# Low halves of the up-projection's weights: from a VectorE subtraction to a ScalarE negation and an accumulating DMA on GpSimd's queue

## The chip, the cores and the metric

The kernel runs on one core of a Trainium2 chip. The metric is the device time of one execution in microseconds (us), less is better. The kernel before takes 1237.1 us, the median of 2 runs (1236.72 to 1237.47).

The engines of a core are named as in the profile: PE (TensorE, the matmuls), PEld (its weight loads), DVE (VectorE), ACT (ScalarE), POOL (GpSimd) and SP (SyncE, which only issues transfers here). Each engine works through its own instructions strictly in order. DMA queues are fed by SP ("SPq"), POOL ("POOLq") and ACT ("ACTq"), and 16 DMA engines move the data.

## The reference

A trunk of two layers on one sequence of 512 tokens with D = 1024: layer 0 mixes tokens with attention with a forget gate, layer 1 with a gated short convolution. Each mixer is followed by the MLP, which is what the change touches, and by a gated embedding.

```python
def sq_relu_mlp(h, w_up, w_down):          # w_up (1024, 4096), w_down (4096, 1024)
    return jnp.square(jax.nn.relu(h @ w_up)) @ w_down

for i in range(DEPTH):                     # DEPTH = 2
    ...
    x = x + rmsnorm(m, g[1])               # m: the mixer's output
    f = sq_relu_mlp(rmsnorm(x, g[2]), w_up[i], w_down[i])
    x = x + rmsnorm(f, g[3])
    ...
```

All inputs and the output are float32.

## The kernel before, in words

**Numbers in two parts.** Every operand of a large matmul is kept as two tiles of the type float32r: hi, the value rounded, and lo, what the rounding left (value minus hi). `mm3` (L262) issues three products for one: hi by hi (L264), lo by hi (L265), hi by lo (L266). `split` (L270) makes the two parts: ScalarE writes hi with a copy that rounds (L272), and an engine, DVE unless told otherwise, writes lo as source minus hi (L273). In the profile L272 is the line of all casts and L273 that of all subtractions; the tiles are told apart by name (wh and wl for weights, hTh and hTl for the normed activations, S1h, A12l and so on for the down-projection's right-hand sides).

**The stream of weights.** All weights come from HBM as tiles of 128x512 float32, 256 KB each, in one planned list. `plan` and its relatives write `loads` (what to load) and `order` (what to prepare). `fetch` (L157) issues the loads on SP's queue into a ring of 14 raw buffers (`RAWS`, tiles "raw"); a buffer can be loaded again when its last reader is done with it. `prepare` (L170) goes through `order`: it fetches the tile, takes two pages (wh, wl) from a pool and calls `split`. `wide` and `narrow` are called by the matmul loops and prepare 8 tiles (`SOON`) ahead.

**The MLP.** For each layer 8 groups of 512 hidden channels. A group has 8 raw tiles of the up-projection (key "up"); there are 128 such tiles in all. `up` makes four blocks f = 0 to 3 of hidden activations: for each, eight steps k with `mm3`, then Relu (L825) and Square on ACT. For groups 0 to 6 the down-projection is computed with seven products instead of eight (`plan_down`, `down`): besides the four quarters B11, B12, B21, B22 of the weight block, it needs the sums T1 to T4 of them, made in `derive` (L167, tiles dn_T) by POOL, eight per group, and the low parts of these sums are also made by POOL (`prepare` chooses `nc.gpsimd` for derived "dn" tiles, so wl<-dn_T at L273). On the other side, `quarters` (L839) has POOL form four sums s of the activations per half group, eight per group, from which ACT and DVE then make S1h, S1l and so on. `down` adds each product onto an accumulator with DVE (L871). `combine` (L878) has POOL add the seven accumulators into the output after group 6, 14 additions per layer, while group 7 ("up" and an ordinary "dn") runs.

**Around the MLP.** The norms: squares on ACT (L295, into "junk"), two small operations on POOL (L287, L290, tiles n_r, cor_r, or_r and mr_r), scaling on DVE (L303, n_h), transposes on PE (L312, n_p), then `split` into hT.

**What sets the order.** The Python order of the statements isn't the order of the engines: the tile framework schedules the whole program by a timeline of its own (`schedule_with_timeline_sim=True`), places each instruction on its engine, and adds the waits between engines. Each engine then runs its list in that order.

Of the kernel before, what the change touches and what calls it, by code (L numbers as in the profile page):

```python
# [11 lines left out]
ALU = mybir.AluOpType  # L12
# [56 lines left out]
def trunk(ctx: ExitStack, tc, x, pT, g, wv, wqk, bf, wo, wci, wcq, cw, wco, wup, wdn, wpp, wpg, out):  # L69
    nc = tc.nc  # L70
# [9 lines left out]
    def page(name, dtype=F32):  # L80
        return pages.tile([P, S], dtype, tag="pg", name=name)
# [69 lines left out]
    def fetch(upto):  # L151
        while len(fetched) < min(upto, len(loads)):
            n = len(fetched)
            raw = raws.tile([P, S], F32, tag="raw", name=f"raw{n}")
            fetched.append(raw)
            src = loads[n]
            nc.sync.dma_start(raw[:, : src.shape[-1]], src)  # L157

    def derive(key):
        at, sums = recipes.pop(key)  # L160
        fetch(max(at.values()) + 1)
        B = {name: fetched[n][:, :S] for name, n in at.items()}
        for name, a, b, op in sums:
            t = page("_".join(str(u) for u in (*key, *name)))
            derived[(*key, *name)] = t
            B[name] = t[:, :S]
            ins = nc.gpsimd.tensor_tensor(out=B[name], in0=B[a], in1=B[b], op=op)  # L167
            if last_norm:
                tc.add_manual_dep(
                    ins.ins, last_norm.pop().ins.name,  # L170
                    mybir.DependencyInfo(mybir.DependencyClass.Sync, mybir.DependencyReason.DATA),
                )

    def prepare(upto):
        while begun[0] < min(upto, len(order)):
            n = begun[0]
            begun[0] += 1
            key, at = order[n]
            for of in (key[:3], key[:2]):
                if of in recipes:  # L180
                    derive(of)
            hi, lo = page(f"wh{n}", F32R), page(f"wl{n}", F32R)
            if isinstance(at, tuple):
                raw, w = derived.pop(key), S
                eng = nc.gpsimd if key[0] == "dn" or key[-1] in ON_POOL else nc.vector
            else:
                fetch(at + 1)
                raw, eng, w = fetched[at], nc.vector, loads[at].shape[-1]
                fetched[at] = None
            split(hi[:, :w], lo[:, :w], raw[:, :w], eng)  # L190
            ready[key] = Pair(hi[:, :w], lo[:, :w])

    def wide(*key, soon=SOON):

        prepare(where[key] + 1 + soon)
        return ready[key]
# [73 lines left out]
    def split(hi, lo, src, eng=nc.vector):  # L270

        nc.scalar.copy(hi, src)  # L272
        eng.tensor_tensor(out=lo, in0=src, in1=hi.bitcast(F32), op=ALU.subtract)  # L273
# [96 lines left out]
    def mixer_out(kind, lhs, xs, gB, then, opened):  # L370


        mgs, sums = {}, {}
        for t, n in BLOCKS:
            if (t, n) == (2, 0):
                prepare(where[kind, 1, KT - 1] + 1 + SOON)
            at = (t, n) in opened
            ps = opened.pop((t, n)) if at else bank(f"{kind}{n}_{t}")
            for k in range(KT - 1 if at else 0, KT):
                mm3(ps, lhs(k, t), wide(kind, n, k, soon=soon(t, n)), k == 0, k == KT - 1)  # L380
            sums[t, n] = squares(ps, f"{kind}s{n}_{t}")
            mgs[t, n] = gained(ps, gB, n, f"{kind}m{n}_{t}")
            if (t, 1 - n) in mgs:
                residual(t, *([d.pop((t, i)) for i in range(2)] for d in (mgs, sums)), xs[t],
                         f"{kind}r")
                then(t)

    def attention(hT, first_x, g0, by_hand):
# [212 lines left out]
        def stream():  # L601
            for i in range(1, KT):
                yield from project(i)
            yield from out_part((0,), range(6))
            yield from out_part((1,), range(6))
            prepare(where["o", 1, KT - 1] + 1)
            yield from out_part((0, 1), (6,))
# [499 lines left out]
```

## Time and profile before

| | |
|---|---|
| median of 2 runs | 1237.1 us |
| span of the profiled execution | 1235.8 us |
| that execution beside the median | 1.3 us shorter (span only) |
| PE busy | 1213.4 us |
| DVE, ACT, POOL busy | 896.5, 676.1, 686.8 us |
| bytes moved by DMA | 148.73 MB |

The numbers of an engine are the time in which it executes. A row of the groups view gives line, engine, operation, output<-inputs, shapes and count, then total busy time and mean ns of one, then the engine's idle time ahead of these instructions and whom it waited for. A row of the timeline gives start and duration in us, and in brackets the idle time before it and its releaser; "x4" is four alike in a row. The waits view gives, for a pair of lines, the time waited in total, how often, and the longest. A row with min/median/max lists the durations in ns of one tile's instructions.

### The profile page before, as it was taken

Reading aid. Unit: us, or ns where it says so; the run is one execution under the profiler, and the core shown is the slowest. Engines: PE = TensorE matmul, PEld = TensorE weight load, DVE = VectorE, ACT = ScalarE, POOL = GpSimd, SP = SyncE. Lnnn points to the kernel's source line nnn. Section 1 sums busy time; section 2 is a strip of 40 time slices with the busy share of each in tenths; the row PEclk is TensorE's granted clock in tenths of the full one; section 3 lists DMA queues with packets and bytes.
Section 4 is the critical chain, followed back from the end, with each engine's and each line's share of the span. In section 5 each row is a group of like instructions: output and inputs, shape, how many; then the busy total and the mean of one; then the engine's idle time right before and its main releaser. Section 6 shows DMA issues by size and latency. Waiting matters only on the chain.

```text
span 1235.8 us, 18684 instructions
## 1 busy us (share of the span) xinstructions
PE 1213.4 (98%) x6188; PEld 1030.6 (83%) x6188; DVE 896.5 (73%) x1394; ACT 676.1 (55%) x1429; POOL 686.8 (56%) x667
## 2 busy tenths in 40 slices
PE   7999999999999999999999999999999999999997
PEld 6888888888888888888889999989778888888885
DVE  5657878675667667869877798865767787669873
ACT  5457777556635654465566544445756345635551
POOL 2016667247878777775213255317778868778210
PEclk9999999999999999999999999999999999999999
DMA  7456564442343224428133033552412443235401
GB/s 253 150 160 169 147 159 114 151 164 66 115 137 98 88 88 136 123 69 288 67 102 107 27 107 96 154 176 71 136 59 78 137 136 95 66 114 178 163 18 52
DMA packets 85793, 148.73 MB, mean 120 GB/s; under 512 B 10112, under 2 KB 17328, under 8 KB 85696
## 3 DMA queue, kind: packets, MB, share of 16 engines
q1 hardware_dynamic: 85488, 147.27, 38.7%
q8 instruction: 49, 0.80, 0.3%
q14 instruction: 48, 0.39, 0.1%
q10 hardware_dynamic: 144, 0.26, 0.1%
q0 software_dynamic: 64, 0.00, 0.0%
HBM read 136.93 MB, written 6.37 MB: 116 GB/s over the span
## 4 chain that ended last, share of the span: by engine, by line
PE 89%; DVE 3%; POOL 2%; ACT 2%; issue 2%; DMA 2%; SPq 0%; POOLq 0%; DVEq 0%; ACTq 0%
PE up L266 9%; PE up L265 9%; PE up L264 9%; PE dn L265 8%; PE dn L266 8%; PE dn L264 8%; PE pg L265 2%; PE pg L264 2%; PE pg L266 2%; PE qk L264 2%; PE qk L265 2%; PE qk L266 2%; PE co L264 1%; PE co L266 1%; PE co L265 1%
## 5 line engine op out<-in xcount | busy, mean ns | idle before, releaser
L273 DVE TENSOR_TENSOR wl<-raw,wh 128x512 fp32r<-128x512 f32 (+1 forms) x398 | 370.2, 975 | 27.5 <-ACT wh L272 26.3
L272 ACT CAST wh<-raw 128x512 fp32r<-128x512 f32 (+1 forms) x398 | 217.1, 620 | 4.6 <-DVE xd L348 4.4
L265 PE MATMUL up<-hTh,wl 128*128 128x512 f32 (+1 forms) x576 | 210.2, 365 | 0.0
L266 PE MATMUL up<-hTl,wh 128*128 128x512 f32 (+1 forms) x576 | 209.7, 366 | 0.3 <-DVE hTl L273 0.3
L264 PE MATMUL up<-hTh,wh 128*128 128x512 f32 (+1 forms) x576 | 209.4, 366 | 0.0
L273 POOL TENSOR_TENSOR wl<-dn_T,wh 128x512 fp32r<-128x512 f32 x112 | 155.0, 1417 | 32.6 <-ACT wh L272 32.6
L825 ACT ACTIVATE r<-up 128x512 f32<-128x512 f32 (+1 forms) x72 | 39.4, 547 | 200.4 <-PE up L266 200.4
L871 DVE TENSOR_TENSOR acc<-dn,acc 128x512 f32<-128x512 f32 x168 | 107.2, 678 | 23.9 <-PE dn L266 23.9
L265 PEld LDWEIGHTS up<-hTh,wl 128*128 128x128 f32 x576 | 108.6, 189 | 17.7
L264 PEld LDWEIGHTS up<-hTh,wh 128*128 128x128 f32 x576 | 108.6, 189 | 17.5
L266 PEld LDWEIGHTS up<-hTl,wh 128*128 128x128 f32 x576 | 108.3, 189 | 17.9 <-DVE hTl L273 0.5
L167 POOL TENSOR_TENSOR dn_T<-raw,raw 128x512 f32<-128x512 f32 x56 | 87.5, 1575 | 58.9 <-DMA raw<-in_wdn 39.6
L167 POOL TENSOR_TENSOR dn_T<-raw,dn_T 128x512 f32<-128x512 f32 x56 | 93.3, 1666 | 2.2
L272 ACT CAST wh<-dn_T 128x512 fp32r<-128x512 f32 x112 | 61.4, 616 | 11.0 <-POOL dn_T L167 11.0
L273 DVE TENSOR_TENSOR A12l<-q,A12h 128x512 fp32r<-128x512 f32 x28 | 23.3, 833 | 51.7 <-ACT A12h L272 51.7
L273 DVE TENSOR_TENSOR A11l<-q,A11h 128x256 fp32r<-128x256 f32 x28 | 25.9, 926 | 45.5 <-ACT A11h L272 45.5
L878 POOL TENSOR_TENSOR acc<-acc,acc 128x512 f32<-128x512 f32 x28 | 46.9, 1706 | 9.9 <-DVE acc L871 9.9
L264 PE MATMUL qk<-hTh,wh 128*128 128x512 f32 x128 | 51.1, 399 | 0.0
L266 PE MATMUL qk<-hTl,wh 128*128 128x512 f32 x128 | 50.8, 397 | 0.0
L265 PE MATMUL pg<-wh,hTl 128*128 128x512 f32 x128 | 50.5, 394 | 0.0
L264 PE MATMUL pg<-wh,hTh 128*128 128x512 f32 x128 | 50.4, 394 | 0.0
L265 PE MATMUL qk<-hTh,wl 128*128 128x512 f32 x128 | 50.2, 393 | 0.0
(372 smaller groups left out, 3240.3 us busy)
## 6 DMA issues: line engine op xcount, KB each, us to landing
raw<-in_wup SPq DMA_DIRECT2D x128, 256.0 KB, 3.0
raw<-in_wdn SPq DMA_DIRECT2D x128, 256.0 KB, 2.9
raw<-in_wcq SPq DMA_DIRECT2D x36, 256.0 KB, 2.9
raw<-in_wqk SPq DMA_DIRECT2D x32, 256.0 KB, 3.6
raw<-in_wpg SPq DMA_DIRECT2D x32, 256.0 KB, 4.0
g<-in_g SPq DMA_DIRECT2D x22, 256.0 KB, 5.8
prl<-neg_c SPq DMA_DIRECT2D x16, 256.0 KB, 7.0
raw<-in_wo SPq DMA_DIRECT2D x16, 256.0 KB, 4.0
```

The lines of the kernel that those rows point to most:

```text
L167: ins = nc.gpsimd.tensor_tensor(out=B[name], in0=B[a], in1=B[b], op=op)
L264: nc.tensor.matmul(ps, a.hi, b.hi, start=start, stop=False)
L265: nc.tensor.matmul(ps, a.lo, b.hi, start=False, stop=False)
L266: nc.tensor.matmul(ps, a.hi, b.lo, start=False, stop=stop)
L272: nc.scalar.copy(hi, src)
L273: eng.tensor_tensor(out=lo, in0=src, in1=hi.bitcast(F32), op=ALU.subtract)
L825: nc.scalar.activation(r[:, :n], ps[:, :n], AF.Relu)
L871: nc.vector.tensor_tensor(out=a, in0=banks[s], in1=a, op=ALU.add)
L878: nc.gpsimd.tensor_tensor(out=a, in0=a, in1=acc[i, s][:, :S], op=ALU.add)
```

## The change

For "up" tiles alone, `prepare` no longer calls `split`. ScalarE writes hi as before and then a second time, into lo, the rounded value of the raw tile's negative. A DMA issued by GpSimd then adds the raw tile onto lo, so that lo becomes raw minus hi.

```diff
-            split(hi[:, :w], lo[:, :w], raw[:, :w], eng)
+            if key[0] == "up":
+                nc.scalar.copy(hi[:, :w], raw[:, :w])
+                nc.scalar.mul(lo[:, :w], raw[:, :w], -1.0)
+                nc.gpsimd.dma_start(lo[:, :w], raw[:, :w], accum_op=ALU.add)
+            else:
+                split(hi[:, :w], lo[:, :w], raw[:, :w], eng)
```

In numbers: 128 subtractions leave DVE, 128 operations come to ACT, 128 DMA issues come to POOL's instruction list, each of one 128x512 tile within SBUF. The matmuls that read a low part of an "up" tile wait for the DMA's landing instead of for DVE, and the raw buffer is free again after that landing. Lines below the edit have numbers higher by 5 in the new file (a matmul of L264 is there L269). The scheduler also places other instructions anew, in particular it interleaves the steps of blocks f = 0 and 1 at the start of a group on PE.

## The prediction

> **What bounds the kernel now.** I read the page's busy shares first, then the chain that ended last, then what TensorE waits for.
>
> ```profile
> span 1235.8 us, 18684 instructions
> PE 1213.4 (98%) x6188; PEld 1030.6 (83%) x6188; DVE 896.5 (73%) x1394; ACT 676.1 (55%) x1429; POOL 686.8 (56%) x667
> ...
> PE 89%; DVE 3%; POOL 2%; ACT 2%; issue 2%; DMA 2%; SPq 0%; POOLq 0%; DVEq 0%; ACTq 0%
> ```
>
> ```profile
> PE g L981 <- DMA row<-in_g: 6.4, 1, 6.4
> ...
> PE dn L264 <- ACT r L825: 1.1, 2, 0.9
> ...
> PE n_p L312 <- DVE n_h L303: 0.8, 1, 0.8
> PE dn L265 <- DVE S1l L273: 0.8, 2, 0.4
> ```
>
> PE is busy for 98%: all its idle time is 1235.8 - 1213.4 = 22.4 us, 6.4 of it at the launch. A gain of 2% is 24.7 us, so no relief of another engine can bring it without taking matmuls away, and the change takes none. The question is only whether something that PE never waited for becomes late. The windows below are one group of the MLP each (eight "up" tiles, then eight "dn"; columns: length, busy and count of PE, PEld, DVE, ACT, POOL, clock, DMA share, GB/s).
>
> ```profile
> 920.84:961.65 40.81, 40.81 (x182) 33.79 (x181) 32.47 (x38) 20.83 (x38) 31.30 (x24) 1.00 0.35 100
> ...
> 1043.20:1084.00 40.80, 40.80 (x181) 33.78 (x180) 28.97 (x37) 20.82 (x38) 30.30 (x24) 1.00 0.36 105
> ```
>
> A group lasts 40.8 us and PE is full in it, at clock 1.00. DVE has about 10 us free, ACT 20, POOL 9.5 to 10.5.
>
> **The change: what leaves DVE.** 128 of the subtractions in this row go (128 "up" tiles: 2 layers, 8 groups, 8 tiles).
>
> ```profile
> L273 DVE TENSOR_TENSOR wl<-raw,wh 128x512 fp32r<-128x512 f32 (+1 forms) x398 | 370.2, 975 | 27.5 <-ACT wh L272 26.3
> L272 ACT CAST wh<-raw 128x512 fp32r<-128x512 f32 (+1 forms) x398 | 217.1, 620 | 4.6 <-DVE xd L348 4.4
> ```
>
> At 975 ns that is 8 x 0.975 = 7.8 us of DVE per group, 125 us in all, every one beside full PE: worth nothing, except in the few waits of PE on DVE quoted above, below 2 us together. DVE's order also lets B22's low parts go behind two more accumulations; DVE's extra slack pays for that.
>
> **What comes to ACT.** 128 negations. Timed by ACT's own train of like casts:
>
> ```profile
> 909.08 7.39 ACT L272 CAST wh<-raw 128x512 fp32r<-128x512 f32 x14
> 928.29 0.60 ACT L825 ACTIVATE r<-up 128x512 f32<-128x512 f32 x1 [11.82 <-PE up L266]
> ```
>
> 7.39 / 14 = 0.53 us each, 4.2 us per group. The train of 14 is followed by 11.82 us of idle time, and the negations are put into that train, so they lie in the gap: nothing. Without that gap they would cost 4.2 us a group. The exception is the start of layer 1, below.
>
> **What comes to POOL.** 128 issues of an accumulating DMA, eight per group, in its in-order stream. In the new order of instructions a steady group on POOL is: issues 0 and 1, one sum dn_T, issues 2 to 4, two dn_T, issues 5 to 7, five dn_T, four s, four wl, four s, four wl. So each issue delays all that follows: the sums, the s that the down-projection's right-hand sides come from, and its low parts wl, which PE needs. POOL's group before (start, duration, and in brackets the idle time ahead of it):
>
> ```profile
> 919.48 1.35 POOL L167 TENSOR_TENSOR dn_T<-raw,raw 128x512 f32<-128x512 f32 x1 [5.84 <-DMA raw<-in_wdn]
> 921.18 1.35 POOL L167 TENSOR_TENSOR dn_T<-raw,raw 128x512 f32<-128x512 f32 x1 [0.35 <-DMA raw<-in_wdn]
> 922.49 3.44 POOL L167 TENSOR_TENSOR dn_T<-raw,dn_T 128x512 f32<-128x512 f32 x2
> ...
> 929.30 3.63 POOL L167 TENSOR_TENSOR dn_T<-raw,dn_T 128x512 f32<-128x512 f32 x2
> 932.89 1.19 POOL L839 TENSOR_TENSOR s<-q 128x256 f32<-128x256 f32 x1
> ...
> 936.45 0.80 POOL L839 TENSOR_TENSOR s<-q,s 128x256 f32<-128x256 f32 x1
> 938.50 5.59 POOL L273 TENSOR_TENSOR wl<-dn_T,wh 128x512 fp32r<-128x512 f32 x4 [1.25 <-ACT wh L272]
> ...
> 947.01 0.74 POOL L839 TENSOR_TENSOR s<-q,s 128x256 f32<-128x256 f32 x1
> 949.01 5.97 POOL L273 TENSOR_TENSOR wl<-dn_T,wh 128x512 fp32r<-128x512 f32 x4 [1.25 <-ACT wh L272]
> 960.78 1.30 POOL L167 TENSOR_TENSOR dn_T<-raw,raw 128x512 f32<-128x512 f32 x1 [5.80 <-DMA raw<-in_wdn]
> ```
>
> ```profile
> L167 POOL TENSOR_TENSOR dn_T<-raw,raw x56: 1276/1496/4144, 273.0 to 1089.2; 128x512 f32<-128x512 f32 x56
> L273 POOL TENSOR_TENSOR wl<-dn_T,wh x112: 1284/1302/1818, 285.0 to 1116.4; 128x512 fp32r<-128x512 f32 x112
> ```
>
> The free time is the 5.8 us ahead of the first dn_T and little else. With near-minimal durations, since DVE now disturbs POOL less (1.7 us apiece while both run, 1.3 alone): eight dn_T at about 1.38 = 11.05, eight wl at 1.30 = 10.4, eight s at 0.78 = 6.2, two waits for ACT's casts = 2.55; together 30.2 us. The eight issues therefore fit into 40.8 us as long as one takes POOL less than (40.8 - 30.2) / 8 = **1.3 us**. Beyond that the kernel's period is POOL's: 30.2 + 8 Ti.
>
> What does an issue take? The trace has two on this queue, of a small transfer:
>
> ```profile
> L972 POOL DMA_DIRECT2D row<-in_g x2: 497/623/749, 1.4 to 2.1; - x2
> ...
> DMA to landing us min/median/max: 4.5/4.7/4.9
> ```
>
> ```profile
> q1 hardware_dynamic: 85488, 147.27, 38.7%
> ...
> q0 software_dynamic: 64, 0.00, 0.0%
> ```
>
> Low end: 0.62 us, if the length of the list does not count. High end: those two left 64 packets, 32 apiece, and a 128x512 tile is at least 128 rows; if time follows packets, 0.62 x 128/32 = 2.5 us, and 2.8 with a few closing packets. I take 1.7, the middle: the page names the queue software's, so a part that grows with rows seems likelier than none, while 0.62 surely holds a fixed part. (Less than nothing is excluded: an issue occupies POOL.)
>
> The sum with 1.7: period 30.2 + 13.6 = 43.8, so +3.0 per steady group. A layer has seven groups with sums; the first two start with POOL rested and with 5.8 us to eat, so 5 x 3.0 x 2 layers = **+30 us**. The eighth group has no sums, but eight issues stand among the closing additions:
>
> ```profile
> 558.92 17.02 POOL L878 TENSOR_TENSOR acc<-acc,acc 128x512 f32<-128x512 f32 x10 [1.90 <-DVE acc L871]
> ```
>
> ```profile
> 586.78 2.48 DVE L921 TENSOR_TENSOR acc<-dn,acc 128x512 f32<-128x512 f32 x4 [1.86 <-PE dn L266]
> ```
>
> The additions end at 575.9 and are read at 586.8: 10.9 us of cover against 13.6 of issues plus what POOL is behind, some +2 per layer, **+4**.
>
> Start of layer 1. Four negations fall among ACT's casts while PE waits for the last norm, a chain that even now makes PE wait 0.8 us (n_p, above):
>
> ```profile
> 827.04 0.62 ACT L272 CAST wh<-raw 128x512 fp32r<-128x512 f32 x1
> ...
> 828.56 0.61 ACT L295 ACTIVATE junk<-co 128x512 f32<-128x512 f32 x1
> ```
>
> ```profile
> 829.35 0.49 POOL L287 TENSOR_SCALAR cor_r_v<-cos,cos 128x1 f32<-128x1 f32 x1 [7.69 <-ACT junk L295]
> ...
> 840.90 0.30 POOL L287 TENSOR_SCALAR n_r_v<-n_q,n_q 128x1 f32<-128x1 f32 x1 [3.17 <-ACT junk L295]
> ```
>
> ```profile
> 250.79 0.30 POOL L287 TENSOR_SCALAR n_r_v<-n_q,n_q 128x1 f32<-128x1 f32 x1 [10.10 <-ACT junk L295]
> ```
>
> Four times 0.53 = **+2.1** on that chain. Of layer 1's first eight issues four stand ahead of the norm operation at 829.35 and four ahead of a later one: 4 x 1.7 = 6.8 us, inside the first gap (7.69), outside the shorter ones: some **+1**. At the start of layer 0 seven issues go into a gap of 10.10 us: 7 x 1.7 = 11.9, **+1.8**. Sum: 30 + 4 + 2.1 + 1 + 1.8 = +39, on the profiled span of 1235.8. The runs' median of 1237.1 stands 1.3 us above that span, since it counts what lies around it; the change adds nothing there. 1237.1 + 39 = **1276 us**.
>
> **The transfers.** Each moves a 256 KB tile from SBUF onto another. Nearest rows for the time to landing: 3.0 us for a 256 KB load and 4.7 for the short row on POOL's queue.
>
> ```profile
> raw<-in_wup SPq DMA_DIRECT2D x128, 256.0 KB, 3.0
> ...
> kh<-kh SPq DMA_DIRECT2D x16, 128.0 KB, 5.1
> ```
>
> I take 6, an estimate above both. POOL is free for issue 0 at 949.01 + 5.97 = 954.98, and PE begins the next group at 961.65 and in the new order puts six products without these low parts first (a product is 40.8/180 = 0.227 us, so 1.4): the first low part is read 8.1 us after its issue can start, later ones, by the same count, after 7 to 8. So 6 is hidden and 9 is not; if nothing hid it, 6 us a group would be 96. The 16 engines have room: a packet now takes 0.387 x 16 x 1235.8 / 85488 = 90 ns; at two to three times that, 8 tiles x 8 packets per engine are 11 to 17 us beside the 14 (0.35) of a group. Raw buffers come free at the landing, not at DVE's subtraction; the loads run a group ahead, so 6 us is covered there too. The new waits of PE on a landing queue nothing but PE's own matmuls.
>
> **The rivals.**
> *A. Cheap issue (the other side: not slower).* An issue takes 1.0 us or less, decided at 1.3. Eight issues of 1.0 then fit beside the 30.2; left are layer 1's 2.1 and about 2 of small delays: 1237 + 4 = 1241. For it: 0.62 in the only row. Against it: that row is of a short list. The Trainium skill, "DMA: Bandwidth & Descriptors" (section "Anatomy of one DMA — SWDGE (gpsimd) path"), speaks for it: descriptor generation is small and "You can emit a lot of descriptors before the incremental cost shows up"; by its fit of 2.0 us plus bytes at 436 GB/s such a transfer is done in an estimated 2.6 us. No trace here shows it for 128 rows, and the 4.7 us to landing of a 2 KB row is already longer than its fixed 2.0.
> *B. Dear issue or late landing.* At Ti 2.5 the period is 50.2: 9.4 x 10 = 94, about 20 at the two closings (eight issues are 20 us against 10.9) and 10 at the starts, +125, 1362. Or landings of 9 to 15 us, because accumulating reads the target first, or transfers queue behind one another: 2 to 8 us of wait per group, x 16 = +32 to +128. For it: 2.5 is the packets' ratio; and 5.1 us for half the bytes from kh to kh. Against it: 3.0 for the loads. Middle: about 1325.
> *C. Relief pays.* The waits of PE on DVE go and POOL, undisturbed, is never late: at most 3 us, 1234. Against it: PE's 98%.
>
> **How the numbers follow.** Two per cent is 25 us, about what a measurement of this kernel is asked to tell from no change. My forecast (Ti 1.3 to 2.2, 1245 to 1310): 0.45, of which 0.08 ends within 2% (Ti below 1.55). A: 0.22. B: 0.30. C: 0.03, which I let stand as the chance of a gain over 2% that I have not seen. Same = 0.22 + 0.08 = 0.30; slower = 0.37 + 0.30 = 0.67; faster = 0.03. The range: from 1239 (inside A, leaving out C and some of A) to 1350 (B without its upper third), with some 2 in 10 outside. The forecast's own range is 1245 to 1310.
>
> **What would show it.** Right: the POOL row of the new line has a mean near 1.7 us; POOL is busy 43 to 44 us of a longer group; the 5.8 us wait ahead of the first dn_T is gone; PE waits for POOL's wl or, through s and ACT's S1h, for POOL, in the "dn" steps. Landing near 6 us and no PE wait of "up" on the DMA. Wrong: a mean below 1.3 (A), above 2.2 or "up" waiting for the landing (B), or a group that stays at 40.8 us.

## The result and the profile after

The changed kernel takes **1267.8 us** (median of 2 runs, 1266.4 to 1269.3) against 1237.1: 1.0244 times as long, 95% interval 1.0227 to 1.026. The profiled execution has a span of 1267.5 us, 31.7 more than the one before. Line numbers from the edit on are higher by 5.

The page after: span, busy shares, the new queue's packets, the shares of the chain that ended last, and the row of the issues.

```profile
span 1267.5 us, 18903 instructions
...
PE 1225.8 (97%) x6188; PEld 1027.9 (81%) x6188; DVE 870.0 (69%) x1266; ACT 741.2 (58%) x1557; POOL 767.0 (61%) x795
...
q0 software_dynamic: 18496, 33.57, 15.8%
...
PE 46%; POOL 9%; issue 7%; DVE 7%; DMA 6%; ACT 4%; POOLq 0%; DVEq 0%; ACTq 0%; SPq 0%
...
L193 POOL DMA_DIRECT2D wl<-raw x128 | 127.2, 1393 | 35.0 <-DVE wl L278 23.1
```

PE was 89% of the chain and is 46% now: other engines and the landings have come onto the path. What PE waits for (total, times, longest):

```profile
PE up L270 <- DMA wl<-raw: 9.3, 10, 1.8
...
PE dn L270 <- DVE S1l L278: 2.5, 5, 0.7
...
PE dn L270 <- DVE A12l L278: 1.7, 2, 1.0
...
PE pg L271 <- DVE wl L278: 1.1, 2, 0.5
PE dn L271 <- POOL wl L278: 0.9, 1, 0.9
```

These are the first low part of an "up" tile that has not landed, and low parts of the down-projection's right-hand sides on VectorE; the pg row is the gate's. For POOL's own products PE waits once, and for S1h, which is made from s, never.

Where the 31.7 us lie, by the starts of PE's matmuls in the timeline of both kernels:

| stretch | before | after | more |
|---|---|---|---|
| start to first "up" of layer 0 | 0 to 262.9 | 0 to 265.2 | 2.3 |
| MLP of layer 0 (first "up" to first "pp") | 335.7 | 344.3 | 8.6 |
| gate and mixer, to first "up" of layer 1 | 235.9 | 241.3 | 5.4 |
| MLP of layer 1 | 334.8 | 347.5 | 12.7 |
| gate of layer 1 and end | 66.5 | 69.3 | 2.8 |

The two MLPs together lose 21.3 us, the other stretches 10.5. After a wait the next products start late too (at 990.03, 990.36 and 990.60 in the case below, where they are otherwise 0.227 us apart). Counted in the starts of PE's products until they are 0.227 us apart again, the landings cost about 12.7 us in the MLPs, A12l and S1l 6.3, where they cost 2.4 before, and POOL's wl 1.2: together 17.8 us more than before, of the 21.3. (The expectations below put the landings at 13.9.)

Two groups of layer 1 as windows (columns as above: length, busy PE, PEld, DVE, ACT, POOL):

```profile
980.80:1025.38 44.58, 41.70 (x181) 33.55 (x180) 29.31 (x28) 27.74 (x52) 36.69 (x33) 1.00 0.63 159
1025.38:1067.10 41.72, 41.32 (x182) 33.63 (x180) 28.44 (x28) 23.70 (x44) 35.88 (x33) 1.00 0.57 140
```

POOL is busy 36 to 37 us: more than before (31), yet less than the 40.8 us that PE's matmuls need. Its list is not too long. The first of these groups shows what happens instead; POOL's timeline:

```profile
976.61 1.77 POOL L193 DMA_DIRECT2D wl<-raw  x2
981.51 1.29 POOL L167 TENSOR_TENSOR dn_T<-raw,raw 128x512 f32<-128x512 f32 x1 [3.13 <-PE up L269]
982.74 2.65 POOL L193 DMA_DIRECT2D wl<-raw  x3
984.42 2.29 POOL L167 TENSOR_TENSOR dn_T<-raw,raw 128x512 f32<-128x512 f32 x1
985.87 2.08 POOL L167 TENSOR_TENSOR dn_T<-raw,dn_T 128x512 f32<-128x512 f32 x1
...
997.93 1.18 POOL L844 TENSOR_TENSOR s<-q 128x256 f32<-128x256 f32 x1
```

and PE's row that ends the wait:

```profile
990.03 0.50 PE L270 MATMUL up<-hTh,wl 128*128 128x512 f32 x1 [1.82 <-DMA wl<-raw]
```

The chain of waits leads back from there (start, duration, what):

```profile
976.05 1.18 DVE wl L278
...
977.24 4.10 DMA raw<-in_wdn
...
981.53 0.52 POOL dn_T L167
982.05 0.48 issue
...
982.74 7.24 DMA wl<-raw
...
990.03 0.50 PE up L270
```

Issues 2 to 4 stand behind the first sum dn_T, which starts only at 981.51. Its bracket names a matmul of PE; the chain names what landed last before it, the raw tile of the down-projection (977.24 + 4.10 = 981.34), whose buffer the subtraction on VectorE at 976.05 had freed. (The median of these loads is 4.1 us on the page, 2.9 before. In e7 below it is 4.0 and next to nothing is lost, so fuller DMA engines alone are not the cause.) So issue 2 comes at 982.74, two us after PE began the group at 980.80, and its landing 7.2 us later is what PE waits for. The sums s begin 17.1 us after the group's start; before it was 12.0 (920.84 to 932.89). Of these 5.1 us, 2.1 are the later start of the first sum (0.7 us after the group's start, before 1.4 us ahead of it), and 3.0 come between it and s. In the other groups from the second on, s begins 15.5 to 19.1 us after the group's start, before 8.8 to 15.0. Two things are also to be read in the issue itself: three issues hold the next instruction up by 984.42 - 982.74 = 1.68 us, 0.56 apiece, and the sum that follows is longer (2.29 against 1.25 to 1.3), as it overlaps the end of the last issue; the sum after it starts 1.45 us later all the same. The view of the line of the issues gives 0.85 us for one at the least:

```profile
L193 POOL DMA_DIRECT2D wl<-raw x128: 850/1178/3244, 241.9 to 1159.6; - x128
...
DMA to landing us min/median/max: 3.3/6.0/14.5
```

### The profile page after: what moved, and what is told of

Same layout as the page of the kernel before. It is cut to its first block, busy times and chain, and to the rows that moved or that the text cites. A ratio compares the mean times of both kernels' runs of the same rounds, so it can differ in the third digit from the quotient of the medians.

```text
span 1267.5 us, 18903 instructions
## 1 busy us (share of the span) xinstructions
PE 1225.8 (97%) x6188; PEld 1027.9 (81%) x6188; DVE 870.0 (69%) x1266; ACT 741.2 (58%) x1557; POOL 767.0 (61%) x795
## 3 DMA queue, kind: packets, MB, share of 16 engines
q0 software_dynamic: 18496, 33.57, 15.8%
## 4 chain that ended last, share of the span: by engine, by line
PE 46%; POOL 9%; issue 7%; DVE 7%; DMA 6%; ACT 4%; POOLq 0%; DVEq 0%; ACTq 0%; SPq 0%
PE up L270 6%; PE up L271 6%; PE up L269 6%; DMA wl<-raw 5%; PE dn L269 4%; PE dn L270 4%; PE dn L271 4%; POOL dn_T L167 2%; POOL wl L278 2%; POOL s L844 2%; ACT junk L300 2%; DVE acc L876 1%; DMA raw<-in_wdn 1%; PE co L269 1%; PE co L270 1%
## 5 line engine op out<-in xcount | busy, mean ns | idle before, releaser
L278 DVE TENSOR_TENSOR wl<-raw,wh 128x512 fp32r<-128x512 f32 (+1 forms) x270 | 323.4, 1241 | 47.3 <-ACT wh L277 42.3
L269 PE MATMUL up<-hTh,wh 128*128 128x512 f32 (+1 forms) x576 | 204.2, 366 | 1.2 <-ACT hTh L277 1.2
L277 ACT CAST wh<-raw 128x512 fp32r<-128x512 f32 (+1 forms) x270 | 150.5, 616 | 6.1 <-DMA raw<-in_wpg 5.3
L193 POOL DMA_DIRECT2D wl<-raw x128 | 127.2, 1393 | 35.0 <-DVE wl L278 23.1
L167 POOL TENSOR_TENSOR dn_T<-raw,raw 128x512 f32<-128x512 f32 x56 | 104.0, 2206 | 39.7 <-DMA raw<-in_wdn 13.4
L167 POOL TENSOR_TENSOR dn_T<-raw,dn_T 128x512 f32<-128x512 f32 x56 | 125.1, 2233 | 1.3
L269 PEld LDWEIGHTS up<-hTh,wh 128*128 128x128 f32 x576 | 108.6, 189 | 19.3 <-ACT hTh L277 1.6
L192 ACT ACTIVATE wl<-raw 128x512 fp32r<-128x512 f32 x128 | 81.6, 637 | 0.0
L278 DVE TENSOR_TENSOR A11l<-q,A11h 128x256 fp32r<-128x256 f32 x28 | 40.0, 1427 | 57.3 <-ACT A11h L277 49.1
L191 ACT CAST wh<-raw 128x512 fp32r<-128x512 f32 x128 | 78.9, 616 | 0.0
L277 ACT CAST S1h<-s 128x512 fp32r<-128x512 f32 x28 | 17.4, 621 | 99.5 <-POOL s L844 99.5
L883 POOL TENSOR_TENSOR acc<-acc,acc 128x512 f32<-128x512 f32 x28 | 52.9, 3899 | 5.8 <-DVE acc L876 5.8
L269 PE MATMUL pg<-wh,hTh 128*128 128x512 f32 x128 | 50.7, 396 | 1.3 <-ACT hTh L277 1.2
L269 PE MATMUL qk<-hTh,wh 128*128 128x512 f32 x128 | 51.1, 399 | 0.0
```

The costliest lines, as they stand in the source:

```text
L191: nc.scalar.copy(hi[:, :w], raw[:, :w])
L192: nc.scalar.mul(lo[:, :w], raw[:, :w], -1.0)
L193: nc.gpsimd.dma_start(lo[:, :w], raw[:, :w], accum_op=ALU.add)
L269: nc.tensor.matmul(ps, a.hi, b.hi, start=start, stop=False)
L883: nc.gpsimd.tensor_tensor(out=a, in0=a, in1=acc[i, s][:, :S], op=ALU.add)
```

## The experiments

Three theories, before the first runs. **Theory 1:** PE waits for landings, since issues queue behind sums that wait. **Theory 2:** POOL's work, lengthened by the issues, comes late for everything behind it. **Theory 3:** the scheduler gave the engines another order, and the order costs. "MLPs" is the length of the two MLP stretches of the table above in the profiled execution (670.5 us before, 691.7 after); "rest" is its span less that (565.3 and 575.8). The profiled execution of e5 is 4.7 us shorter than the median, that of e3 2.9 longer; in the others the two lie within 1.5 us.

| kernel | median us | ratio to before (95%) | MLPs | rest |
|---|---|---|---|---|
| e1 negation only | 1240.3 | 1.0014 to 1.0033 | 673.8 | 564.8 |
| e2 plain copy | 1262.9 | 1.0191 to 1.0233 | 686.0 | 574.4 |
| e3 last group split | 1262.7 | 1.0181 to 1.0215 | 687.6 | 576.3 |
| e4 low parts on DVE | 1250.6 | 1.0087 to 1.0117 | 675.0 | 574.1 |
| e5 order held | 1260.1 | 1.0154 to 1.0206 | 676.8 | 576.9 |
| e6 DMA beside | 1296.1 | 1.0457 to 1.0492 | 719.7 | 574.5 |
| e7 copy from SP | 1240.3 | 1.0013 to 1.0033 | 672.7 | 565.1 |
| e8 two more raws | 1266.8 | 1.022 to 1.025 | 690.2 | 575.1 |
| e9 order put alone | 1240.9 | 1.0019 to 1.0039 | 668.3 | 570.3 |
| e10 DMA in last only | 1243.1 | 1.0035 to 1.0065 | 671.4 | 571.5 |
| e11 order held, last split | 1254.8 | 1.0127 to 1.0157 | 677.7 | 575.6 |
| e12 all three | 1246.0 | 1.0057 to 1.0091 | 670.1 | 573.3 |

**e1.** The negation without the DMA:

```diff
-                nc.gpsimd.dma_start(lo[:, :w], raw[:, :w], accum_op=ALU.add)
+                nc.vector.tensor_tensor(out=lo[:, :w], in0=raw[:, :w], in1=lo[:, :w].bitcast(F32), op=ALU.add)
```

> ScalarE's part alone: hi and the negative are written as in the changed kernel, but VectorE adds the raw tile onto lo; no DMA is issued by GpSimd. Times go by 1237.1 us before and 1267.8 us changed. Every theory that blames the DMA (its landing, GpSimd's issue time, contention) expects 1236 to 1240 us, with DVE busy as before. If ScalarE's 128 further operations, or the other order that the scheduler makes of them, cost something by themselves, the time is 1245 us or more.

1240.3 us, at the upper end of what the theories that blame the DMA expect, and 3 us over before. So ScalarE's part is nearly free, and some 28 of the 31 us belong to the DMA and to the order that the scheduler makes with it.

**e2.** The same stream, without the addition:

```diff
-                nc.gpsimd.dma_start(lo[:, :w], raw[:, :w], accum_op=ALU.add)
+                nc.gpsimd.dma_start(lo[:, :w], raw[:, :w])
```

> The same kernel as the changed one, instruction for instruction in the same order, but the DMA copies the raw tile onto lo and adds nothing (so lo holds the raw value, and the subtraction is left out). Theory 1, waits for landings: if the landing falls from 6.0 us to 4 because nothing is read back from the target, the 13.9 us that PE loses on landings shrink to a few and the time is 1253 to 1258 us; if the landing stays at 6, the time stays at 1266 to 1269. Theory 2, GpSimd's issue time: the issue takes the same, 1266 to 1269.

1262.9 us, between the two expectations. Its issues and landings, its packets, and PE's waits:

```profile
L193 POOL DMA_DIRECT2D wl<-raw x128: 530/530/635, 240.9 to 1153.3; - x128
...
DMA to landing us min/median/max: 2.3/4.1/8.1
```

```profile
q0 software_dynamic: 18496, 33.57, 8.5%
```

```profile
PE dn L270 <- DVE A12l L278: 3.1, 7, 0.5
PE dn L270 <- DVE S1l L278: 3.1, 8, 0.4
PE up L270 <- DMA wl<-raw: 2.9, 3, 1.5
```

The landing fell from 6.0 to 4.1 us and the waits for it to 2.9, as theory 1 says; but the time fell by 5 us only, since waits for A12l and S1l came up in place of them: the groups of this kernel are 42.2 us long, one after the other. Landings alone are refuted as the cause: whatever makes A12l late is there with the shortest issues too. One of these groups, which starts at 476.5, shows it:

```profile
475.14 1.29 POOL L167 TENSOR_TENSOR dn_T<-raw,raw 128x512 f32<-128x512 f32 x1 [6.49 <-DMA raw<-in_wdn]
...
504.33 5.51 POOL L278 TENSOR_TENSOR wl<-dn_T,wh 128x512 fp32r<-128x512 f32 x4 [1.25 <-ACT wh L277]
```

```profile
505.03 1.29 DVE L876 TENSOR_TENSOR acc<-dn,acc 128x512 f32<-128x512 f32 x2 [6.27 <-PE dn L271]
506.23 1.20 DVE L278 TENSOR_TENSOR A12l<-q,A12h 128x512 fp32r<-128x512 f32 x1
```

POOL is not late here: it rests for 6.49 us ahead of its first sum, and its second four wl begin 27.8 us after the group's start, against 27.3 in the steady groups before. What is new is the place of A12l. It stands behind two accumulations that wait for PE and starts at 29.7 us instead of 23.9, so it runs beside POOL's wl and takes 1.20 us instead of 0.69. The kernel before has this order in one group of each layer, without any issue; in layer 1 it looks like this, and PE waits 0.37 us for A12l and 0.39 for S1l:

```profile
907.22 1.29 DVE L871 TENSOR_TENSOR acc<-dn,acc 128x512 f32<-128x512 f32 x2 [4.98 <-PE dn L266]
908.43 1.11 DVE L273 TENSOR_TENSOR A12l<-q,A12h 128x512 fp32r<-128x512 f32 x1
```

In the changed kernel PE waits for A12l in just the two groups in which POOL's second four wl have begun by then (those from 980.80 and 1067.1). In the others POOL is later, A12l takes 0.68 to 0.87 us, and PE does not wait for it.

**e3.** `if key[0] == "up" and key[2] < 14:` in the changed kernel.

> The last group of each layer (16 of 128 tiles) goes back to VectorE's subtraction. Theory 3, order: the 6.5 us lost between the start of group 6 and the end of the down-projection and the 5.8 us lost in the gate matmuls come from the order that the scheduler gives the last group, and all 12 go: 1254 to 1257 us. Theories 1 and 2 count an eighth of the landings or issues: 1263 to 1265 us.

1262.7 us, 5 less for an eighth of the tiles: near theories 1 and 2. The closing's part is small, and what the gate loses is mostly still there.

**e4.** Low parts of the sums on VectorE:

```diff
-                eng = nc.gpsimd if key[0] == "dn" or key[-1] in ON_POOL else nc.vector
+                eng = nc.gpsimd if key[-1] in ON_POOL else nc.vector
```

> The changed kernel, with the 112 low parts of the down-projection's sums moved from GpSimd to VectorE, which takes 10.4 us per group off GpSimd. Theory 2 (GpSimd's list is too long): GpSimd is rested, the sums s come on time, and what PE loses on S1l, A12l and wl goes, 1252 to 1258 us. Theory 1 (landings behind a sum that waits for its load): those waits stay, 1262 to 1268 us. If VectorE is slowed by GpSimd (its subtractions take 2.8 us apiece beside the issues), more work on it costs more: over 1268 us.

1250.6 us, 17 less than the changed kernel, with the same 128 issues and the changed order on VectorE. POOL and VectorE in one group:

```profile
504.55 0.88 POOL L193 DMA_DIRECT2D wl<-raw  x1 [5.14 <-ACT wl L192]
...
514.79 1.29 POOL L167 TENSOR_TENSOR dn_T<-raw,raw 128x512 f32<-128x512 f32 x1 [6.25 <-DMA raw<-in_wdn]
```

```profile
501.33 1.29 DVE L876 TENSOR_TENSOR acc<-dn,acc 128x512 f32<-128x512 f32 x2 [4.89 <-PE dn L271]
502.54 0.68 DVE L278 TENSOR_TENSOR A12l<-q,A12h 128x512 fp32r<-128x512 f32 x1
```

POOL waits for ACT now and issues four tiles 10 us ahead of the first sum; the landings no longer wait for anything (PE's waits for them: 0.7 us in all). And A12l takes 0.68 us. In the changed kernel, where POOL writes the low parts wl at that moment, the same step reads:

```profile
1011.47 1.29 DVE L876 TENSOR_TENSOR acc<-dn,acc 128x512 f32<-128x512 f32 x2 [4.68 <-PE dn L271]
1012.67 1.40 DVE L278 TENSOR_TENSOR A12l<-q,A12h 128x512 fp32r<-128x512 f32 x1
```

VectorE waits for PE, adds two products, and only then makes the A12l that PE waits for next: with 0.7 us more in that ring, PE stops (at 1014.13 it has waited 0.66 us). Theory 2 said 1252 to 1258, and the time is a little below that. But the edit does two things: it rests POOL, so that issues come early, and it takes the wl away from beside A12l. It does not tell POOL's lateness from this overlap. It does show that VectorE's spare time is of use, though for other work than the change gave it.

**e5.** The order of VectorE held, in `down` (`ins` is the accumulation, `lows` holds the last S1l of the group; the lines that fill them are left out):

```diff
+                        if lows and i in STEPS[:3]:
+                            tc.add_manual_dep(
+                                ins.ins, lows[0].ins.name,
+                                mybir.DependencyInfo(mybir.DependencyClass.Sync, mybir.DependencyReason.DATA),
+                            )
```

> The changed kernel, with a dependency that holds the accumulations of the first three products of a group on VectorE behind the low part S1l of f = 3, so that VectorE's order at this place is again that of the kernel before (A11l, A12l, S1l, then accumulations). Theory 3 in its new form, order: PE's waits for A12l and S1l (1.4 us in each group, 42.23 against 40.8 in the run with the plain copy) go, some 14 us of the 31, and the waits for landings stay: 1252 to 1257 us. If the lateness of GpSimd and not the order causes these waits, the time stays at 1264 to 1269.

The MLPs lose 6.4 us instead of 21.3, and every group from the third on is exactly 40.8 us long with all eight issues in it. POOL in one of them:

```profile
1010.96 2.64 POOL L193 DMA_DIRECT2D wl<-raw  x3
1015.67 1.29 POOL L167 TENSOR_TENSOR dn_T<-raw,raw 128x512 f32<-128x512 f32 x1 [2.08 <-DMA raw<-in_wdn]
1016.92 3.54 POOL L193 DMA_DIRECT2D wl<-raw  x4
```

It even waits 2.08 us. So the issues do fit, and PE waits for A12l and S1l no more. But more than VectorE's order is new: the scheduler also put three issues ahead of the first sum instead of two, and PE's waits for landings fell from 9.3 us to 2.2, which the expectation had not foreseen. (2.9 us of waits for the held accumulations came instead.) The gain of the whole is smaller (1260.1, runs from 1255.4 to 1263.1; the profiled one is the shortest): theory 3's range began at 1252, and the gate and mixer got longer than in any other of the kernels that were profiled in this series, by one wait of 3.9 us for a norm among other things. Both readings of the expectation are missed in total; within the MLPs it is theory 3's.

**e6.** VectorE keeps its subtraction; negation and DMA go to a spare page:

```diff
+                split(hi[:, :w], lo[:, :w], raw[:, :w], eng)
+                beside = page(f"beside{n}", F32R)
+                nc.scalar.mul(beside[:, :w], raw[:, :w], -1.0)
+                nc.gpsimd.dma_start(beside[:, :w], raw[:, :w], accum_op=ALU.add)
```

> The kernel before with VectorE's subtraction kept; ScalarE's negative and GpSimd's accumulating DMA go to a page of their own that nothing reads. PE waits for no landing, but GpSimd issues 128 times, VectorE has its full work, and the scheduler gives VectorE the changed order. Theory 1 (PE's waits for landings are the cause): 1240 to 1245 us. Theories 2 and 3 (GpSimd's lateness, order): the 13.9 us of landing waits are gone, the rest stays or grows with VectorE's work: 1252 to 1262 us.

1296.1 us: worse than every theory said. PE waits for no landing here, and still:

```profile
PE up L271 <- DVE wl L279: 16.0, 4, 7.0
PE dn L272 <- POOL wl L279: 11.9, 15, 1.1
```

So the issues do harm without a landing on PE's path, which theory 1 alone does not explain, and POOL's own wl is late 15 times, which is theory 2. In the changed kernel, where VectorE has less work, that happens once. The 16.0 us are VectorE's 128 subtractions coming late in the last group; my expectation had left out that raw buffers are then held by two readers. How that part arises in detail was not followed.

**e7.** The copy on SyncE's queue:

```diff
-                nc.gpsimd.dma_start(lo[:, :w], raw[:, :w], accum_op=ALU.add)
+                nc.sync.dma_start(lo[:, :w].bitcast(F32), raw[:, :w])
```

> As the plain copy (lo holds the raw value, the subtraction is left out), but issued on SyncE's queue: GpSimd issues nothing, and VectorE's order is that of the kernel before. Theories 2 and 3: groups of 40.8 us and 1238 to 1243 us. Theory 1: the landing, 4.1 us in the plain copy, still comes behind ScalarE's negative and keeps PE waiting, 1247 us or more.

1240.3 us. The same bytes move inside SBUF and land as late (median 4.2 us), PE's products depend on them just as well, and against e2 22.6 us are gone with POOL's issues, and with the other order that the scheduler makes for them (VectorE's is that of the kernel before):

```profile
PE up L270 <- DMA wl<-raw: 1.2, 1, 1.2
```

**e8.** `RAWS = 16`, `PAGES = 69`.

> The changed kernel with 16 raw buffers instead of 14 (and 69 pages instead of 70), so that the next down-projection tiles are loaded earlier and GpSimd's first sum does not wait for them. Theory 1, with the landing late because issues 2 to 4 stand behind that sum: the landing waits fall from 13.9 us to below 5 and the time to 1256 to 1260 us. If issues are late because GpSimd's list before them is late, nothing changes: 1265 to 1269 us.

1266.8 us. The waits for landings fell from 9.3 to 6.0 us, those for A12l and S1l rose from 4.2 to 8.9, and the time did not move. With the loads earlier POOL is earlier too, and its wl come to stand beside A12l: in all eight groups in which PE waits for A12l it takes 1.35 to 1.79 us. One wait went and the other came.

**e9.** The reverse of e5, on the kernel before: A12l and S1l of f = 3 are emitted after the first accumulations and made to wait for them by the same kind of dependency.

> The kernel before, with no DMA from GpSimd and no negation, but VectorE held to the changed kernel's order in groups 1 to 6: the first two accumulations of a group ahead of A12l of f = 3, a third ahead of S1l. If the order by itself costs, PE waits for A12l and S1l in every group as in the plain copy (1.4 us in each of 12, less the one group of each layer that has it already): 1249 to 1255 us. If the order only hurts when GpSimd is late with its eight issues, 1237 to 1241 us.

1240.9 us, and the MLPs are 2 us shorter than before. VectorE's order put in this way costs nothing there. But the scheduler put six other products on PE between the two steps, 1.4 us of cover for A12l, which takes about 1.0 to 1.25 us in most of these groups. So this is not the full order of the changed kernel, and the run does not show that its order is harmless without issues; the group of the kernel before, under e2, has 0.8 us of waits with it. The rest is 5.0 us longer, with no DMA of this kind in the kernel; e10's rest is 6.2 longer. In both, and in the changed kernel, PE waits in the same four places of the gate and mixer (for za, twice for a weight's low part, for a norm), 3.3 us in all, where the kernel before waits 0.7. In e1 and e7, whose order in the last stretch on PE is that of before, the rest is not longer. About half of the 10.5 that the changed kernel loses outside the MLPs is thus what rescheduling the gate and mixer costs even without the change.

**e10.** `if key[0] == "up" and key[2] >= 14:`.

> The accumulating DMA for the last group's 16 tiles alone; groups 0 to 6 as before, with the order of before. If eight issues among the closing additions are what the ends of the MLP lose (3.3 us to the end of the down-projection and 2.9 in the gate matmuls, per layer): 1247 to 1251 us. If the ends lose because the groups ahead of them left GpSimd late, 1237 to 1242 us.

1243.1 us, a little above the second expectation, with MLPs 0.9 us longer. So the closing hardly suffers from its own issues; what it loses in the changed kernel seems to come with the groups before it. What is left over is the rescheduling of e9.

**e11.** e5 and e3 together.

> The order held as in e5 and the last group split by VectorE as in e3. If the groups lose by order and the ends by the issues in the closing, both go and 1240 to 1246 us are left: what remains is the first groups' landing waits, about 2 us, and the mixer. If the two don't add, it stays near e5's 1260.

1254.8 us, between the two expectations. The median is 5 us less than e5's, as e3's was 5 less than the changed kernel's, but e5's runs spread over 7.7 us, and in the profiled executions the MLPs are no shorter than e5's. So it is not shown that the two add. The MLPs keep 7.3 us, in the first groups of layer 1 and in the closings.

**e12.** e11 and e4 together.

> Order held (e5), last group split by VectorE (e3) and the sums' low parts on VectorE (e4), with 112 accumulating DMAs left. If lateness of GpSimd is what still costs in e11 (waits for its wl and the late closing), 1241 to 1247 us: the 5 us that gate and mixer lose in every rescheduled kernel, e9 included, stay. If what e11 has left is of another kind, 1252 to 1256 us.

1246.0 us, within the first range: the MLPs are at 670.1, where they were before the change. (As in e4, POOL's wl are also gone from beside VectorE.) What is left lies in the rest, 8.0 us longer than before. No version with the DMA comes below the kernel before, and none could by much, as PE's idle time is 22.4 us.

**What stands.** The loss comes with issuing the DMA on POOL and the order that the scheduler makes for it, not with the negations (e1) or with the bytes moved (e7). In the MLPs of the changed kernel it reaches PE in two ways. Landings are late, about 12.7 us, because issues 2 to 7 stand behind sums, the first of which waits for its load; where a third issue goes ahead of that sum (e5) or four do (e4), most of it goes. And A12l and S1l are late on VectorE, because the scheduler's order puts them behind accumulations that wait for PE, and so beside POOL's wl: holding the old order (e5) or taking the wl off POOL (e4) ends these waits. For this second part the lateness of POOL, theory 2, is not needed (e2, and one group before the change); it shows in e6, and in the changed kernel in a single wait of 0.9 us. Not shown is what the changed kernel's order on PE and VectorE together would cost in all groups without issues, as e9 came out with another order on PE. Open too are how e6's last group loses 16 us, and the other half of what the gate and mixer lose.

## Why the prediction came out right, and where its steps were wrong

- *What bounds the kernel, and that VectorE's relief is worth nothing*: right. DVE fell from 896.5 to 870.0 us only, as its other subtractions grew longer, and PE gained nothing.
- *ScalarE's negations lie in a gap*: right (e1). Of the 2.1 us for the start of layer 1 nothing is seen ahead of it in e1 (gate and mixer 235.9 us, as before); its first group is 1.0 us longer (46.1 against 45.1), which need not be the negations: with all of them e12 has 45.1.
- *An issue takes POOL 1.7 us, between 0.62 and 2.5*: mis-sized by three. It holds the stream up by 0.56 and lies at the low end (the row's mean of 1.39 us overlaps what follows it); the number of rows hardly counts (530 ns for a plain copy of 128 rows, 497 to 749 for the short row). The prediction's period with 0.6 is 30.2 + 8 x 0.6 = 35.0 us, near the 35.9 for which POOL was busy. By its own criterion of 1.3 us the 30 us of the steady groups should then have been nothing, and rival A should have won at 1241.
- *"Beyond that the kernel's period is POOL's: 30.2 + 8 Ti"*: this is the step that failed. It makes POOL's list longer than a group, and +30 us hang on it. The groups did get longer (41.2 to 44.6 us from the second to the sixth, before 39.4 to 43.1), but POOL was busy for 36 to 37 us of the two shown and waited 3.1 and 4.3 us ahead of their first sums. The sums s came later, as the path from the sums to s has no idle time (the row of two dn_T at 929.30 ends at 932.93, the first s starts at 932.89), but PE never waited for S1h and once for POOL's wl. In place of a full POOL the runs show the two waits named above, for landings and for A12l and S1l.
- *"DVE's order also lets B22's low parts go behind two more accumulations; DVE's extra slack pays for that"*: the new order was looked at for B22 alone. That A12l and S1l go behind accumulations as well was put at nothing; they cost 6.3 us, 2.4 before, and in e2 they are more than half of what the MLPs lose.
- *Landing 6, hidden*: the 6.0 was right, the cover was not. It counted from the time at which POOL is free for issue 0 and left out that issues 2 to 4 stand behind a sum that waits itself: about 12.7 us, where the sum had nothing. "Up" waiting for the landing was one of its own signs of being wrong.
- *Closings +4, starts +5*: the MLPs with the closings lost 21.3 where 34 was forecast; start and mixer lost 10.5 where 5 was, about half of it the rescheduling (e9, e10), which the prediction did not consider.
- *Rivals*: A was right in the price of an issue and wrong in what follows from it. B's landing waits were there, but smaller than its 2 to 8 us per group (12.7 / 16 = 0.8), and with a landing of 6, not 9. C's relief paid nothing. So it is luck that the time lies only 8.2 us below the forecast: an issue three times too dear made up for waits that the sum had at nothing.

In the Trainium skill, "DMA: Bandwidth & Descriptors" (section "Anatomy of one DMA — SWDGE (gpsimd) path") says that generating descriptors is small and grows late with their number: the issue rows agree. Its fit would have the transfer done in an estimated 2.6 us; the median landings of 6.0 and 4.1 us are longer (the shortest plain copy took 2.3), and the measurement decides.

## What to carry to other kernels

When work is added to an engine that runs in order, don't stop at comparing the sum of its list with the period. Ask of each added piece what it stands behind, and when its result is needed: here issues stood behind a sum that waited for a load, on an engine with idle time to spare. And where a scheduler sets the order, part of a change's price is the order that it makes of it, on the other engines too: look for steps that moved behind a wait or beside another engine's work. Holding the old order at the one place where a wait shows up is a cheap test, but read the new order of all engines before saying what it shows.

## What the runs showed of the hardware

- An accumulating DMA's packets take twice as long: 0.158 x 16 x 1267.5 / 18496 = 173 ns against 0.085 x 16 x 1260.4 / 18496 = 93 ns for the plain copy of the same tiles, and it lands after 6.0 instead of 4.1 us. Its issue alone takes 850 ns against 530.
- The issue of the accumulating kind overlaps the next instruction of POOL, and both rows grow: dn_T had a mean of 1.6 us before, 2.2 after, 1.47 beside plain copies. Most of that is overlap: behind the issues of 982.74, the two sums hold POOL for 1.45 and 1.23 us from their start to that of the next instruction.
- VectorE's subtractions of two SBUF tiles can grow beside POOL's: A12l 0.68 us alone, 1.40 beside POOL's wl. The Trainium skill, "SBUF — State Buffer" (section "Who interferes with whom"), says that a VectorE instruction with two SBUF inputs contends with a GpSimd instruction that reads SBUF; these rows agree.
